# One decoder layer on one core: attention probabilities and the merged sum transposed by VectorE in blocks and through memory

## The chip, the core and the metric

One core of a Trainium2 chip runs the kernel. The metric is the time of one execution on the device in microseconds. The kernel before takes 324.86 us (median of three runs, 324.63 to 325.22).

## The reference

One layer over x (256 tokens, width 1024) with a memory of 256 tokens, all in float32:

```python
h = rms_norm(x, norm_g)
(qa, ka, va, ga, ub, vb, gb, qc, gc, ma, mb, mc) = split_cols(h @ w_in, IN_SPLITS)
out_a = moba_attention(rope(qa), rope(ka), va) * silu(ga)
out_b = gmlp_spatial_gate(ub, vb, ln_g, w_spatial, b_spatial) * silu(gb)
out_c = memory_cross_attention(qc, rms_norm(mem, mem_norm_g), w_mem_kv) * silu(gc)
y = sigmoid(ma) * (out_a @ w_branch_a) + sigmoid(mb) * (out_b @ w_branch_b) + sigmoid(mc) * (out_c @ w_branch_c)
return rms_norm(x + y @ w_out, final_norm_g)
```

Branch a has six heads of 128; with 256 tokens its block-sparse attention is plain causal attention. Branch b normalises vb and mixes it over tokens with a lower triangular matrix for each of six groups in chunks of 128 tokens, and adds a bias. Branch c has four heads that attend to the 256 memory tokens.

## The kernel before

**Chunks.** The weights come as 106 chunks of 128x1024, two to a piece, from three buffers `raw` on SP's DMA queue (`load`, L172). ScalarE makes the high part of a chunk (`hi`, L184) and VectorE the low part (`lo`, L188), three chunks ahead of TensorE, in four buffers of each. TensorE takes three passes (high by high, high by low, low by high) for a chunk. Chunks 0 to 81 are the input projection: `vvb` and `mv` (values), `sig` (the merge gates, four chunks for each 512 columns: sig 1024 and sig 1536 among them), which give token-major sums (L344 to L346), and q, k, gc, ga, ub, qc, mk, gb, which give feature-major ones (L435). Then come 16 chunks of the branch projections and 8 of the output projection.

**PSUM.** Eight banks: four `acc` and four `aux` (`bank`, L149). The sums of a chunk group lie in two acc banks, but those of vvb 1024 and sig 1024 in two aux banks (L366). Scores, transposes, products with V and the spatial mix take one aux bank each.

**Order.** Everything beside the chunks is a unit of the class `Units` (L68): a name, an engine, a duration in us, a function, the units it comes after, a time to wait before its result counts, and a due chunk. `slot` puts a unit into the program ahead of or behind a chunk once the modelled times say that it is ready. So a changed duration or dependency moves the work of all engines.

**Attention.** A head's scores are computed feature-major (`a_scores`, `c_scores`), softmax is done with probabilities `p` (tokens by keys), and the product with V wants them transposed. For heads 0, 1, 4 and 5 of branch a three 128x128 blocks are transposed by TensorE into an aux bank (`a_pT`, L579), for c head 3 four. For heads 2 and 3 of a (`TURN`) and c 0 to 2 VectorE does it in 16 instructions of 32 rows each (`turn_rows`, L571) into `mid`, a buffer in SBUF that the rope uses before. ScalarE then makes `pth` (L662, L771), VectorE `ptl` (L352), and TensorE multiplies (L674). One diagonal block of a needs no low part and is copied to `pt` (L667).

**Around it.** The rope moves q and k by SP's DMAs (L558). The spatial mix of branch b (`mix_unit`, L814) is three units of eight matmuls, each with a bias add on VectorE (`mix_bias`, L822) and then a product on GpSimd. GpSimd also multiplies ub by its gate (L480). The gates of c and a end as `lo` parts of their outputs (L834). The merged sum y, two halves of 512 columns, is transposed by TensorE, 16 blocks (`y_units`, L579), and split. The norm factors of memory go through a diagonal matrix and two matmuls (L288) to a row broadcast on all partitions.

Of the kernel before, what the change touches and what calls it, by code (L numbers as in the profile page):

```python
# [127 lines left out]
def tile_hybrid_layer(ctx: ExitStack, tc: tile.TileContext, xw, memT, mem, x, fin_g, ln_g, w, w_sp, b_sp, rope, out):  # L128
# [439 lines left out]
    def turn_rows(dst, src, a):  # L568

        for b in range(4):  # L570
            nc.vector.transpose(dst(slice(32 * b, 32 * b + 32), slice(32 * a, 32 * a + 32)),  # L571
                                src(slice(32 * a, 32 * a + 32), slice(32 * b, 32 * b + 32)))
# [80 lines left out]
    def a_turn(h, a):
        p = ST["a", h][0][:, 0:384].rearrange("p (m s) -> p m s", m=3)
        ST["ap", h] = V["mid"][:, TURN.index(h), :]
        pt = ST["ap", h][:, 0:384].rearrange("p (m s) -> p m s", m=3)
        turn_rows(lambda r, s: pt[r, :, s], lambda r, s: p[r, :, s], a)

    def a_pT_out(h):
        ps = ST["ap", h]  # L660
        pth = p_tiles("a", h, ps)
        nc.scalar.activation(pth[:, 0:S], ps[:, 0:S], AF.Copy)  # L662
        if h in TURN:
            ST["a1", h] = ps[:, S:S + 128]
            return
        ST["a1", h] = work.tile([128, 128], F32, name="pt1", tag="pt1", bufs=2)
        nc.scalar.activation(ST["a1", h], ps[:, S:S + 128], AF.Copy)  # L667

    def a_pv(h):
# [4 lines left out]
        nc.tensor.matmul(ps[:, 128:256], V["v1"][:, hsl(h)], ST["a1", h], start=False, stop=True)  # L674

    def a_out(h):
        nc.scalar.activation(V["qk"][:, h, 0, :], ST["ao", h][:, 0:S], AF.Copy)
# [21 lines left out]
            (DVE, 0.2, lambda: nc.vector.reciprocal(lrs, lrt)), after=["vvb.1024"])  # L699

    U.add("sqrts", None, 0, lambda: None, after=["lnr", "mrow"])
    U.chain("mrms", *rms_all("m", rstm), after=["mrow"])
    mk0 = chunks.index(("fea", "mk", 0))

    def mem_units():
        U.add("mxa", None, 0, mem_alloc, after=["vvb.1024"])
        for k in range(KD):
# [3 lines left out]
            U.add(f"mxl{k}", DVE, 0.5, lambda k=k, g=g: gain_lo(mem_k(k), g, V["mh"][:, k, :], V["ml"][:, k, :]),  # L711
                  after=[f"mxh{k}"], due=mk0 - 5 + k // 2)

    for h in range(HA):
        if h == 2:
            mem_units()
        if h % 2 == 0:
            r = h // 2
            U.add(f"rin{r}", QUEUE, 1.6, lambda r=r: rope_move(r, False), wait=1.2,
                  after=[f"{n}{i}" for i in (h, h + 1) for n in "qk"] + ["consts"] + ([f"rout{r - 1}"] if r else []))  # L720
            U.add(f"rp{r}", DVE, 1.65, lambda r=r: rope_pair(r), after=[f"rin{r}"])
            U.add(f"rout{r}", QUEUE, 1.6, lambda r=r: rope_move(r, True), after=[f"rp{r}"], wait=1.2)
# [6 lines left out]
        turn = [(DVE, 1.1, lambda h=h, a=a: a_turn(h, a)) for a in range(4)] if h in TURN else \  # L729
            [(PE, 0.33, lambda h=h: a_pT(h))]  # L730
        U.chain(f"ap{h}", *turn, (ACT, 0.42 if h in TURN else 0.72, lambda h=h: a_pT_out(h)),
                after=[f"an{h}"] + back("v", h))
        U.chain(f"av{h}", (DVE, 0.42, lambda h=h: p_lo("a", h, S)), (PE, 0.55, lambda h=h: a_pv(h)),
                (ACT, 0.4, lambda h=h: a_out(h)), after=[f"ap{h}"])
# [26 lines left out]
    def c_turn(h, a):
        if h == 0 and a == 0:
            V["ct"] = V["mid"]
        p = ST["c", h][0].rearrange("p (t m s) -> p m t s", t=2, m=2)
        pt = V["ct"][:, h, :].rearrange("p (m t s) -> p m t s", t=2, m=2)
        turn_rows(lambda r, s: pt[r, :, :, s], lambda r, s: p[r, :, :, s], a)
        ST["cp", h] = V["ct"][:, h, :]
# [348 lines left out]
```

## Time and profile before

| | |
|---|---|
| median of three runs | 324.86 us (324.63 to 325.22) |
| the profiled execution | 325.27 us |
| its span | 323.3 us |
| TensorE busy | 315.8 us, 98% |
| VectorE busy | 246.6 us, 76% |
| ScalarE busy | 202.5 us, 63% |
| GpSimd busy | 40.1 us, 12% |
| DMA | 64.92 MB, 201 GB/s |

All stands for one profiled execution, whose span lies 1.97 us within its time. [...] In a chain of waits each piece is followed back to what released it.

### The profile page before, as it was taken

To read this page: it belongs to the slowest core of one execution; us is meant where nothing else is said; L and a number is where in the kernel's file an instruction comes from. 1 tells how busy PE (TensorE), PEld (TensorE's weight loads), DVE (VectorE), ACT (ScalarE), POOL (GpSimd) and SP (SyncE) were. 2 spreads that over 40 slices of the span, in tenths; PEclk is the share of its full clock that TensorE was granted. 3 is DMA by queue.
4 is the path that set the end of the run, shared out by engine and by line. 5 is a ranking of instruction groups with operands and counts; after the bars stand their busy time and mean duration, and the time that the engine had idled before them with its cause. 6 is when DMAs were issued, how large, how long until landed. Compare 5 with 4: busy or idle time off the path is not lost.

```text
span 323.3 us, 4570 instructions
## 1 busy us (share of the span) xinstructions
PE 315.8 (98%) x1644; PEld 268.9 (83%) x1644; DVE 246.6 (76%) x419; ACT 202.5 (63%) x346; POOL 40.1 (12%) x42
## 2 busy tenths in 40 slices
PE   8999999999999999999999999999999999999992
PEld 3788888888888888898888888888888888888982
DVE  3969956985876999898979639989857659769452
ACT  4879887556865555557677698576746633434433
POOL 1007420000000000030200009200124000000022
PEclk9999999999999999999999999999999999999999
DMA  7999796555327565554544533864640667463003
GB/s 246 419 426 398 258 363 220 216 194 216 136 78 302 172 180 208 164 192 138 185 151 176 195 130 131 312 233 170 208 182 19 244 231 289 150 241 130 0 2 130
DMA packets 13846, 64.92 MB, mean 201 GB/s; under 512 B 1792, under 2 KB 2944, under 8 KB 8576
## 3 DMA queue, kind: packets, MB, share of 16 engines
q1 hardware_dynamic: 13536, 64.31, 55.1%
q10 hardware_dynamic: 288, 0.33, 0.3%
q8 instruction: 13, 0.21, 0.2%
q14 instruction: 9, 0.07, 0.1%
HBM read 62.79 MB, written 1.05 MB: 197 GB/s over the span
## 4 chain that ended last, share of the span: by engine, by line
PE 96%; DMA 2%; ACT 1%; SPq 0%; ACTq 0%; issue 0%; DVE 0%
PE acc L435 36%; PE acc L344 13%; PE acc L345 13%; PE acc L346 13%; PE aux L344 5%; PE aux L345 5%; PE aux L346 5%; PE acc L375 3%; DMA st<-in_xw_dram 2%; PE aux L579 1%; PE aux L814 1%; PE aux L626 0%; PE aux L674 0%; SPq L218 0%; ACT hi L315 0%; PE aux L288 0%
## 5 line engine op out<-in xcount | busy, mean ns | idle before, releaser
L188 DVE TENSOR_TENSOR lo<-raw,hi 128x1024 fp32r<-128x1024 f32 x102 | 130.2, 1280 | 43.0 <-ACT hi L184 42.0
L184 ACT ACTIVATE hi<-raw 128x1024 fp32r<-128x1024 f32 x102 | 107.6, 1056 | 44.3 <-PE acc L346 29.6
L435 PE MATMUL acc<-n,hi 128*128 128x512 f32 x304 | 78.5, 394 | 0.0
L435 PEld LDWEIGHTS acc<-n,hi 128*128 128x128 f32 x304 | 54.8, 189 | 9.5
L435 PEld LDWEIGHTS acc<-n,lo 128*128 128x128 f32 x304 | 41.5, 190 | 3.0
L435 PE MATMUL acc<-n,lo 128*128 128x256 f32 x304 | 42.4, 282 | 0.0
L344 PE MATMUL acc<-hi,n 128*128 128x512 f32 x80 | 31.5, 394 | 0.0
L345 PE MATMUL acc<-lo,n 128*128 128x512 f32 x80 | 31.2, 390 | 0.0
L346 PE MATMUL acc<-hi,n 128*128 128x512 f32 x80 | 31.2, 389 | 0.0
L571 DVE STREAM_TRANSPOSE mid<-p 32x128 f32<-32x128 f32 (+1 forms) x80 | 23.1, 289 | 1.6 <-ACT p L609 0.5
L741 POOL TENSOR_TENSOR vb<-vb,lng 128x768 f32<-128x768 f32 x2 | 4.6, 2276 | 108.4 <-DMA raw<-in_w_dram 94.7
L346 PEld LDWEIGHTS acc<-hi,n 128*128 128x128 f32 x80 | 15.0, 188 | 3.2
L345 PEld LDWEIGHTS acc<-lo,n 128*128 128x128 f32 x80 | 15.0, 188 | 2.9
L344 PEld LDWEIGHTS acc<-hi,n 128*128 128x128 f32 x80 | 15.0, 188 | 2.9
L958 POOL TENSOR_TENSOR xk<-xk,fing 128x512 f32<-128x512 f32 (+1 forms) x4 | 4.0, 1013 | 68.0 <-ACT jk L954 68.0
L516 POOL TENSOR_TENSOR st<-st,bc 128x256 f32<-128x256 f32 x8 | 9.1, 1170 | 24.4 <-ACT bc L293 24.4
L439 ACT ACTIVATE qk<-acc 128x256 f32<-128x256 f32 x12 | 4.6, 380 | 10.7 <-PE acc L435 10.6
L439 ACT ACTIVATE jt<-acc 128x256 f32<-128x256 f32 x14 | 5.3, 377 | 9.0 <-PE acc L435 8.9
L825 POOL TENSOR_TENSOR qk<-qk,ga 128x512 f32<-128x512 f32 x3 | 5.8, 1966 | 33.8 <-ACT ga L801 33.8
L375 PE MATMUL acc<-hi,h 128*128 128x512 f32 (+1 forms) x34 | 8.9, 386 | 0.9 <-ACT hi L315 0.9
L344 PE MATMUL acc<-hi,a 128*128 128x512 f32 x24 | 9.4, 393 | 0.0
L346 PE MATMUL acc<-hi,a 128*128 128x512 f32 x24 | 9.3, 389 | 0.0
(233 smaller groups left out, 601.2 us busy)
## 6 DMA issues: line engine op xcount, KB each, us to landing
raw<-in_w_dram SPq DMA_DIRECT2D x39, 1024.0 KB, 4.9
raw<-in_w_dram SPq DMA_DIRECT2D x24, 512.0 KB, 4.6
st<-in_xw_dram SPq DMA_DIRECT2D x6, 384.0 KB, 7.2
xk<-in_x_dram SPq DMA_DIRECT2D x2, 1024.0 KB, 9.1
mt<-in_memT_dram SPq DMA_DIRECT2D x2, 512.0 KB, 7.8
mm<-in_mem_dram SPq DMA_DIRECT2D x2, 512.0 KB, 9.8
out_dram<-xk SPq DMA_DIRECT2D x4, 256.0 KB, 2.7
fing<-in_fin_g_dram SPq DMA_DIRECT2D x1, 512.0 KB, 6.9
```

The lines of the kernel that those rows point to most:

```text
L184: nc.scalar.activation(hi[c][:, a:b], raw[c // 2][:, o + a:o + b], AF.Copy)
L188: nc.vector.tensor_tensor(lo[c][:, a:b], raw[c // 2][:, o + a:o + b], hi[c][:, a:b].bitcast(F32), OP.subtract)
L344: nc.tensor.matmul(p, s_hi, m_hi, start=first, stop=False)
L345: nc.tensor.matmul(p, s_hi, m_lo, start=False, stop=False)
L346: nc.tensor.matmul(p, s_lo, m_hi, start=False, stop=last)
L375: nc.tensor.matmul(acc[name, o][t][:, a:b], src[:, k, tsl(t)], wt[c][:, i * 512 + a:i * 512 + b], start=k + n == 0, stop=k == KD - 1 and n ...
L435: nc.tensor.matmul(o, wt, m, start=i == 0, stop=i == len(passes) - 1)
L439: nc.scalar.activation(dst, pa, AF.Copy)
L516: U.add(f"nm{k}", POOL, 1.05, lambda k=k: nc.gpsimd.tensor_tensor(x_k(k), x_k(k), bc["x"], OP.mult), after=["xrms"], due=7)
L571: nc.vector.transpose(dst(slice(32 * b, 32 * b + 32), slice(32 * a, 32 * a + 32)), src(slice(32 * a, 32 * a + 32), slice(32 * b, 32 * b + ...
L741: nc.gpsimd.tensor_tensor(V["vb"][:, t, :], V["vb"][:, t, :], V["lng"], OP.mult)
L825: nc.gpsimd.tensor_tensor(src, src, g, OP.mult)
```

## The change

All ten heads, memory's norm factors and three quarters of y are transposed without TensorE. `turn_blocks` is one VectorE instruction that transposes every 32x32 block in place of its row of blocks; `turn_write` writes the result in four DMAs from SP to a scratch tensor in memory, in runs of 32n floats, in the order that completes the transpose; `turn_read` reads it back by one DMA that ScalarE issues. The result has its columns in another order, which `turn_view` undoes when `pth` and `ptl` are made. The third block of an a head is read straight from there, without a copy. All heads share one buffer for the write, `mid[:, 0]`, one after another (`moved`), and two for the read. The first half of y and one of two token tiles of the second go the same way; the other tile takes four TensorE transposes. The norm factors are written as a row and read back as a broadcast. Pieces 31 and 32 come in halves too, the rope's modelled waits go from 1.2 to 2.4 and 1.6, and the due time of the c scores is gone.

```diff
-        parts = 2 if 20 <= j < 31 else 1
+        parts = 2 if 20 <= j < 33 else 1
...
+    def rms_write(name, r):
+        bc["r" + name] = row = dram.tile([S], F32, name="row" + name)
+        nc.sync.dma_start(bass.AP(tensor=row.tensor, offset=row.offset, ap=[[1, 128], [128, 2]]), r)
+
+    def rms_read(name):
+        bc[name] = work.tile([128, S], F32, name="bc", tag="ssq", bufs=2)
+        nc.sync.dma_start(bc[name], rows(bc["r" + name], S))
...
+    def turn_blocks(dst, src):
+        nc.vector.transpose(dst, src.rearrange("p (u b j) -> p b u j", b=4, j=32))
+
+    def turn_write(name, src, n):
+        ST["d" + name] = d = dram.tile([128, 128 * n], F32, name="turn" + name)
+        w = 32 * n
+        for a in range(4):
+            nc.sync.dma_start(bass.AP(tensor=d.tensor, offset=d.offset + a * w, ap=[[4 * w, 32], [128 * w, 4], [1, w]]),
+                              src[32 * a:32 * a + 32].rearrange("p (b w) -> p b w", b=4))
+
+    def turn_read(name, dst):
+        nc.scalar.dma_start(dst, ST["d" + name])
+
+    def turn_view(t, a, b):
+        return t.rearrange("p (a u i) -> p u a i", a=4, i=32)[:, a:b]
...
-    TURN = (2, 3)
+    TURN_A, TURN_C = (0, 1, 2, 3, 4, 5), (0, 1, 2, 3)
...
-    U.chain("mrms", *rms_all("m", rstm), after=["mrow"])
+    U.add("mrmw", QUEUE, 0.4, lambda: rms_write("m", rstm), after=["mrow"], wait=9.0)
+    U.add("mrms", QUEUE, 0.4, lambda: rms_read("m"), after=["mrmw"], wait=4.0)
...
+    def turn_units(kind, h, n, i):
+        name = f"{kind}{h}"
+        before = [f"{kind}n{h}"] + moved[0]
+        U.add(f"tt{name}", DVE, 0.2 + 0.13 * n, lambda: p_turn(kind, h, n), after=before)
+        U.add(f"tw{name}", QUEUE, 1.6, lambda: turn_write(name, V["mid"][:, 0, 0:128 * n], n), after=[f"tt{name}"], wait=3.6)
+        U.add(f"{kind}pt{h}", ACT, 0.45, lambda: p_back(kind, h, n), after=[f"tw{name}"] + back("v", i), wait=3.2)
+        moved[0] = [f"tw{name}"]
...
-                after=[f"qcl{h | 1}", f"mkl{h | 1}", "sqrts"] + back("p", HA + h), due=n_in - 26 + h)
+                after=[f"qcl{h | 1}", f"mkl{h | 1}", "sqrts"] + back("p", HA + h))
...
-                for i in range(2):
-                    y_units(half, i, [f"y{c}"])
+                if half == 0:
+                    part = y_turn(0, [0, 1], [f"y{c}"], ("yw0", "ub"), ("yr0", "gc"), 4.0)
+
+                    U.add("yp0", ACT, 1.3, part, after=["yr0"], due=n_br - 2)
+                else:
+                    y_turn_pe([f"y{c}"])
+                    V["ylast"] = y_turn(1, [1], [f"y{c}"], ("yw1", "ub"), ("yr1", "gc"), 2.0)
```

Over the whole program TensorE has 1600 matmuls in place of 1630 (four transposes in place of 32, two in place of four for norm factors), VectorE 351 instructions in place of 418, and SP 164 in place of 112.

**TensorE around the spatial mix.** Before, the last matmuls of a chunk of sig 1536, the mix, and the next chunk (`aux_2485`, `aux_2490`, `aux_2495` are the three groups' banks, `wsp` the spatial weights):

```order
L344 MATMUL acc_2472<-hi_2386,n_168 128x512
L345 MATMUL acc_2472<-lo_2387,n_168 128x512
L346 MATMUL acc_2472<-hi_2386,n_168 128x512
L814 MATMUL aux_2485<-wsp_161,vb_284 128x128 [waits Pool_49] x2
L814 MATMUL aux_2485<-wsp_161,vb_284 128x128 x2
L814 MATMUL aux_2490<-wsp_161,vb_284 128x128 x4
L814 MATMUL aux_2495<-wsp_161,vb_284 128x128 [waits Activation_49]
L814 MATMUL aux_2495<-wsp_161,vb_284 128x128 x3
L344 MATMUL acc_2471<-hi_2410,n_168 128x512
```

Now, the mix behind the third chunk of sig 1024 (`aux_2192` and `aux_2193` hold its sums; `aux_2253`, `aux_2258` and `aux_2263` are the mix's):

```order
L353 MATMUL aux_2193<-hi_2159,n_170 128x512
L354 MATMUL aux_2193<-lo_2160,n_170 128x512
L355 MATMUL aux_2193<-hi_2159,n_170 128x512
L877 MATMUL aux_2253<-wsp_163,vb_286 128x128 [waits Pool_49] x2
L877 MATMUL aux_2253<-wsp_163,vb_286 128x128 x2
L877 MATMUL aux_2258<-wsp_163,vb_286 128x128 x4
L877 MATMUL aux_2263<-wsp_163,vb_286 128x128 [waits DVE_49,PE_49]
L877 MATMUL aux_2263<-wsp_163,vb_286 128x128 x3
L353 MATMUL aux_2192<-hi_2186,n_170 128x512 [waits Activation_49]
```

The mix moved from the sums of sig 1536, in acc banks, into those of sig 1024, in aux banks, and the third group's first matmul waits for VectorE in place of ScalarE.

**VectorE around the bias adds of the mix.** Before (`lo` are low parts of weight chunks, `ptl` those of probabilities, `mt` the bias adds):

```order
L188 TENSOR_TENSOR lo<-raw,hi 128x1024
L834 TENSOR_TENSOR ocl<-oc,och 128x512
L188 TENSOR_TENSOR lo<-raw,hi 128x1024 x2
L352 TENSOR_TENSOR ptl<-aux,pth 128x512
L822 TENSOR_TENSOR mt_2501<-aux,bsb 128x256 x2
L822 TENSOR_TENSOR mt_2504<-aux,bsb 128x256 x2
L822 TENSOR_TENSOR mt_2507<-aux,bsb 128x256 x2
L188 TENSOR_TENSOR lo<-raw,hi 128x1024
```

Now (`a` are the low parts of branch a's gated outputs):

```order
L189 TENSOR_TENSOR lo<-raw,hi 128x1024
L897 TENSOR_TENSOR a<-qk,a 128x2x256 x3
L189 TENSOR_TENSOR lo<-raw,hi 128x1024 x2
L361 TENSOR_TENSOR ptl<-mid,pth 128x256 x4
L885 TENSOR_TENSOR mt_2272<-aux,bsb 128x256 x2
L885 TENSOR_TENSOR mt_2275<-aux,bsb 128x256 x2
L189 TENSOR_TENSOR lo<-raw,hi 128x1024
L885 TENSOR_TENSOR mt_2315<-aux,bsb 128x256 x2
```

The first two groups' bias adds now stand behind three chunks' low parts, those of branch a's outputs and the four of c heads 2 and 3; before, they stood behind one c head's low part.

**ScalarE around heads 0 and 1 of branch a.** Before (`gc` are copies out of the gc chunks, `pth` the high parts of probabilities, `qk` the outputs of heads):

```order
L184 ACTIVATE hi<-raw 128x1024
L439 ACTIVATE gc<-acc 128x256
L662 ACTIVATE pth<-aux 128x256
L667 ACTIVATE pt_898<-aux 128x128
L184 ACTIVATE hi<-raw 128x1024
L439 ACTIVATE gc<-acc 128x256
L662 ACTIVATE pth<-aux 128x256
L667 ACTIVATE pt_931<-aux 128x128
L184 ACTIVATE hi<-raw 128x1024
L439 ACTIVATE gc<-acc 128x256
L677 ACTIVATE qk<-aux 128x256 x2
```

Now, three gc chunks further on:

```order
L185 ACTIVATE hi<-raw 128x1024
L448 ACTIVATE gc<-acc 128x256
L594 DMA mid<-turna_946 128x384
L185 ACTIVATE hi<-raw 128x1024
L448 ACTIVATE ub<-acc 128x256
L641 ACTIVATE qh<-qk 128x384 x2
L698 ACTIVATE pth<-mid 128x256
L185 ACTIVATE hi<-raw 128x1024
L448 ACTIVATE ub<-acc 128x256
```

The high part of head 0 stood right behind the first gc copy; now the first of the reads (`mid<-turna`) stands behind the fourth, and the high part of head 0 after one more chunk, with high parts of weight chunks in front and behind.

## Rows read from the trace of the kernel before

**Rows 1.** Table by stretch: us, PE, PEld, DVE, ACT, POOL busy, clock, DMA share, GB/s.

```profile
17.00:312.00 295.00, 295.00 (x1551) 253.70 (x1550) 231.06 (x388) 186.99 (x314) 36.32 (x31) 1.00 0.55 197
```

**Rows 2.** Chain of waits: start us, us, engine, tile, line, count.

```profile
63.66 0.24 PE aux L288 x2
63.91 8.38 PE acc L435 x48
81.82 0.33 PE aux L579 x3
163.04 0.65 PE aux L579 x6
235.09 0.44 PE aux L579 x4
277.11 0.87 PE aux L579 x8
```

**Rows 3.** Timeline, TensorE, 200 to 202 us: start us, us, then the group.

```profile
200.81 0.40 PE L344 MATMUL aux<-hi,n 128*128 128x512 f32 x1
201.96 0.39 PE L346 MATMUL aux<-hi,n 128*128 128x512 f32 x1
```

**Rows 4.** Timeline, TensorE, 237 to 242 us.

```profile
238.14 2.84 PE L814 MATMUL aux<-wsp,vb 128*128 128x128 f32 x24
240.74 0.48 PE L344 MATMUL acc<-hi,n 128*128 128x512 f32 x1
```

**Rows 5.** Timeline, VectorE, 191 to 211 us; in brackets idle before and releaser.

```profile
194.28 1.50 DVE L188 TENSOR_TENSOR lo<-raw,hi 128x1024 fp32r<-128x1024 f32 x1 [1.03 <-ACT hi L184]
196.03 2.00 DVE L188 TENSOR_TENSOR lo<-raw,hi 128x1024 fp32r<-128x1024 f32 x1
204.03 1.22 DVE L188 TENSOR_TENSOR lo<-raw,hi 128x1024 fp32r<-128x1024 f32 x1
205.17 2.98 DVE L834 TENSOR_TENSOR a<-qk,a 128x512 fp32r<-128x512 f32 x3
208.07 3.49 DVE L188 TENSOR_TENSOR lo<-raw,hi 128x1024 fp32r<-128x1024 f32 x3
```

**Rows 6.** Timeline, VectorE, about 165 and 239 us.

```profile
165.13 0.75 DVE L352 TENSOR_TENSOR ptl<-aux,pth 128x256 fp32r<-128x256 f32 x2
239.23 2.54 DVE L822 TENSOR_TENSOR mt<-aux,bsb 128x256 f32<-128x256 f32 x6 [0.27 <-PE aux L814]
```

**Rows 7.** Timeline, GpSimd, 185 to 210 us.

```profile
193.38 5.81 POOL L825 TENSOR_TENSOR qk<-qk,ga 128x512 f32<-128x512 f32 x3 [33.78 <-ACT ga L801]
199.17 3.53 POOL L480 TENSOR_TENSOR ub<-ub,jt 128x512 f32<-128x512 f32 x2
205.46 1.53 POOL L480 TENSOR_TENSOR ub<-ub,jt 128x512 f32<-128x512 f32 x1 [2.76 <-ACT jt L479]
```

**Rows 8.** Groups by line and shape, VectorE, line 571: total us, mean ns, idle before.

```profile
L571 DVE STREAM_TRANSPOSE mid<-p 32x128 f32<-32x128 f32 x48 | 14.5, 302 | 0.7
L571 DVE STREAM_TRANSPOSE mid<-p 32x96 f32<-32x96 f32 x32 | 8.6, 270 | 0.9 <-ACT p L609 0.5
```

**Rows 9.** DMA issues (ns min/median/max) and landings (us), lines 558 and 218; a DMA row.

```profile
L558 SPq DMA_DIRECT2D mid<-qk x12: 507/555/1064, 48.4 to 112.2; - x12
DMA to landing us min/median/max: 1.7/3.3/6.0
L218 ACTq DMA_DIRECT2D st<-in_xw_dram x2: 414/432/451, 0.8 to 1.2; - x2
st<-in_xw_dram ACTq DMA_DIRECT2D x1, 192.0 KB, 3.6
```

**Rows 10.** Waits of SP's queue: total us, times, longest us.

```profile
SPq L170 <- DVE lo L188: 156.4, 33, 9.8
```

**Rows 11.** Timeline, TensorE, 97 to 99 us, two groups of scores.

```profile
97.49 0.38 PE L626 MATMUL aux<-qk 128*128 128x128 f32 x2
98.64 1.54 PE L435 MATMUL acc<-n,hi 128*128 128x512 f32 x6
```

More of the change, by code (lines that the diff above doesn't have):

```diff
@@ L134, in tile_hybrid_layer @@
     work = ctx.enter_context(tc.tile_pool(name="work", bufs=2))
+    dram = ctx.enter_context(tc.tile_pool(name="dram", bufs=1, space=bass.MemoryType.DRAM))
     psum = ctx.enter_context(tc.tile_pool(name="psum", bufs=1, space=PSUM))
@@ L566, in rope_pair @@
         nc.vector.tensor_tensor(x, x, sh, OP.add)
[L568 to L572, printed above, removed]
-    TURN = (2, 3)
+    def turn_blocks(dst, src):
[11 more added lines that the diff above has]
+    TURN_A, TURN_C = (0, 1, 2, 3, 4, 5), (0, 1, 2, 3)
     def transpose4(p, blocks):
@@ L651, in a_pT, with p_turn, p_back, p_lo_turned @@
         transpose4(ST["ap", h], [p[:, hsl(j)] for j in range(3)])
[L653 to L657, printed above, removed]
+    def p_turn(kind, h, n):
+        turn_blocks(V["mid"][:, 0, 0:128 * n].rearrange("p (b u j) -> p b u j", b=4, j=32),
+                    ST[kind, h][0][:, 0:128 * n])
+    def p_back(kind, h, n):
+        t = V["mid"][:, 1 + h % 2, 0:128 * n]
+        turn_read(f"{kind}{h}", t)
+        ST[kind + "p", h] = t
+    def p_lo_turned(kind, h, n):
+        ps, pth, ptl = ST[kind + "T", h]
+        sub_lo(ptl[:, 0:128 * n].rearrange("p (u a i) -> p u a i", a=4, i=32), turn_view(ps, 0, n),
+               pth[:, 0:128 * n].rearrange("p (u a i) -> p u a i", a=4, i=32))
     def a_pT_out(h):
@@ L661, in a_pT_out @@
         pth = p_tiles("a", h, ps)
+        if h in TURN_A:
+            nc.scalar.activation(pth[:, 0:S].rearrange("p (u a i) -> p u a i", a=4, i=32), turn_view(ps, 0, 2),
+                                 AF.Copy)
+            ST["a1", h] = turn_view(ps, 2, 3)[:, 0]
+            return
         nc.scalar.activation(pth[:, 0:S], ps[:, 0:S], AF.Copy)
-        if h in TURN:
-            ST["a1", h] = ps[:, S:S + 128]
-            return
         ST["a1", h] = work.tile([128, 128], F32, name="pt1", tag="pt1", bufs=2)
@@ L673, in a_pv @@
         mm3(ps[:, 0:S], v0[:, 0, hsl(h)], v0[:, 1, hsl(h)], pth[:, 0:S], ptl[:, 0:S], True, False)
-        nc.tensor.matmul(ps[:, 128:256], V["v1"][:, hsl(h)], ST["a1", h], start=False, stop=True)
+        p1, o1 = ST["a1", h], ps[:, 128:256]
+        if h in TURN_A:
+            o1 = o1.rearrange("p (a i) -> p a i", a=4)
+        nc.tensor.matmul(o1, V["v1"][:, hsl(h)], p1, start=False, stop=True)
     def a_out(h):
@@ L712, in mem_units @@
                   after=[f"mxh{k}"], due=mk0 - 5 + k // 2)
+    moved = [[]]
+    def turn_units(kind, h, n, i):
[5 more added lines that the diff above has]
+        moved[0] = [f"tw{name}"]
     for h in range(HA):
@@ L718, in tile_hybrid_layer @@
             r = h // 2
-            U.add(f"rin{r}", QUEUE, 1.6, lambda r=r: rope_move(r, False), wait=1.2,
+            U.add(f"rin{r}", QUEUE, 1.6, lambda r=r: rope_move(r, False), wait=2.4,
                   after=[f"{n}{i}" for i in (h, h + 1) for n in "qk"] + ["consts"] + ([f"rout{r - 1}"] if r else []))
             U.add(f"rp{r}", DVE, 1.65, lambda r=r: rope_pair(r), after=[f"rin{r}"])
-            U.add(f"rout{r}", QUEUE, 1.6, lambda r=r: rope_move(r, True), after=[f"rp{r}"], wait=1.2)
+            U.add(f"rout{r}", QUEUE, 1.6, lambda r=r: rope_move(r, True), after=[f"rp{r}"], wait=1.6)
         U.chain(f"qsl{h}", (ACT, 0.5, lambda h=h: a_split_hi(h)), (DVE, 0.55, lambda h=h: a_split_lo(h)),
@@ L728, in tile_hybrid_layer @@
                 after=[f"as{h}"])
[L729 to L733, printed above, removed]
+        if h in TURN_A:
+            turn_units("a", h, 3, h)
+        else:
+            U.add(f"apt{h}", PE, 0.33, lambda h=h: a_pT(h), after=[f"an{h}"])
+        U.add(f"ap{h}", ACT, 0.42 if h in TURN_A else 0.72, lambda h=h: a_pT_out(h), after=[f"apt{h}"] + back("v", h))
+        low = (lambda h=h: p_lo_turned("a", h, 2)) if h in TURN_A else (lambda h=h: p_lo("a", h, S))
+        U.chain(f"av{h}", (DVE, 0.42, low), (PE, 0.55, lambda h=h: a_pv(h)),
                 (ACT, 0.4, lambda h=h: a_out(h)), after=[f"ap{h}"])
@@ L759, in c_pT, with c_lo @@
         transpose4(ST["cp", h], [p[:, hsl(j)] for j in (0, 2, 1, 3)])
[L761 to L767, printed above, removed]
     def c_pT_out(h):
         ps = ST["cp", h]
-        nc.scalar.activation(p_tiles("c", h, ps), ps, AF.Copy)
+        pth = p_tiles("c", h, ps)
+        if h in TURN_C:
+            for m in range(2):
+                nc.scalar.activation(pth[:, m * S:m * S + S].rearrange("p (u a i) -> p u a i", a=4, i=32),
+                                     turn_view(ps, 0, 4)[:, m::2], AF.Copy)
+            return
+        nc.scalar.activation(pth, ps, AF.Copy)
+    def c_lo(h):
+        if h not in TURN_C:
+            return p_lo("c", h, 512)
+        ps, pth, ptl = ST["cT", h]
+        for m in range(2):
+            o, i = (x[:, m * S:m * S + S].rearrange("p (u a i) -> p u a i", a=4, i=32) for x in (ptl, pth))
+            sub_lo(o, turn_view(ps, 0, 4)[:, m::2], i)
     def c_pv(h):
@@ L788, in tile_hybrid_layer @@
                 (ACT, 1.15, lambda h=h: softmax_exp("c", h)),
-                after=[f"qcl{h | 1}", f"mkl{h | 1}", "sqrts"] + back("p", HA + h), due=n_in - 26 + h)
+                after=[f"qcl{h | 1}", f"mkl{h | 1}", "sqrts"] + back("p", HA + h))
         U.chain(f"cn{h}", (DVE, 0.2, lambda h=h: softmax_sum("c", h)), (ACT, 0.85, lambda h=h: softmax_norm("c", h)),
                 after=[f"cs{h}"])
-        turn = [(DVE, 1.25, lambda h=h, a=a: c_turn(h, a)) for a in range(4)] if h < 3 else             [(PE, 0.44, lambda h=h: c_pT(h))]
-        U.chain(f"cp{h}", *turn, (ACT, 0.62, lambda h=h: c_pT_out(h)), after=[f"cn{h}"] + back("v", HA + h))
-        U.chain(f"cv{h}", (DVE, 0.68, lambda h=h: p_lo("c", h, 512)), (PE, 0.72, lambda h=h: c_pv(h)),
+        if h in TURN_C:
+            turn_units("c", h, 4, HA + h)
+        else:
+            U.add(f"cpt{h}", PE, 0.44, lambda h=h: c_pT(h), after=[f"cn{h}"])
+        U.add(f"cp{h}", ACT, 0.75, lambda h=h: c_pT_out(h), after=[f"cpt{h}"] + back("v", HA + h))
+        U.chain(f"cv{h}", (DVE, 0.84, lambda h=h: c_lo(h)), (PE, 0.72, lambda h=h: c_pv(h)),
                 (ACT, 0.4, lambda h=h: c_out(h)), after=[f"cp{h}", "mvl0", "mvl1"])
@@ L879, in tile_hybrid_layer, with y_parts, y_turn, blocks @@
     BR = [("a", k) for k in range(HA)] + [("b", k) for k in range(GB)] + [("c", k) for k in range(HC)]
-    def y_units(half, i, after):
-        k = slice(4 * half + 2 * i, 4 * half + 2 * i + 2)
+    def y_parts(half, ts, src):
+        k, s = slice(4 * half, 4 * half + 4), slice(128 * ts[0], 128 * ts[-1] + 128)
+        h, l = (V[n][:, k, s].rearrange("p k (t a i) -> p k t a i", t=len(ts), a=4) for n in ("yh", "yl"))
+        for t in range(len(ts)):
+            nc.scalar.activation(h[:, :, t], src[:, :, t], AF.Copy)
+            nc.vector.tensor_tensor(l[:, :, t], src[:, :, t], h[:, :, t].bitcast(F32), OP.subtract)
+    def y_turn(half, ts, after, to, back, us):
+        n = 4 * len(ts)
+        shape = [128, 4, len(ts), 128]
+        def blocks():
+            slot_tile(to[0], shape, to[1])
+            for i, t in enumerate(ts):
+                turn_blocks(V[to[0]][:, :, i, :].rearrange("p b (u j) -> p b u j", j=32), sig[half][:, t, :])
+        def write():
+            turn_write(f"y{half}", V[to[0]].rearrange("p b t x -> p (b t x)"), n)
+        def read():
+            slot_tile(back[0], shape, back[1])
+            turn_read(f"y{half}", V[back[0]].rearrange("p a t x -> p (a t x)"))
+        U.add(f"yw{half}", DVE, 0.75 * len(ts), blocks, after=after)
+        U.add(f"yx{half}", QUEUE, 1.6, write, after=[f"yw{half}"], wait=us)
+        U.add(f"yr{half}", ACT, 0.45, read, after=[f"yx{half}"], wait=3.2)
+        return lambda: y_parts(half, ts, V[back[0]].rearrange("p a t (k i) -> p k t a i", i=32))
+    def y_turn_pe(after):
         def turn():
-            ST["y", half, i] = bank()
-            transpose4(ST["y", half, i], [sig[half][:, t, hsl(2 * i + a)] for a in range(2) for t in range(2)])
-            split2(ST["y", half, i].rearrange("p (k s) -> p k s", k=2), V["yh"][:, k, :], V["yl"][:, k, :])
+            ST["y"] = bank()
+            transpose4(ST["y"], [sig[1][:, 0, hsl(k)] for k in range(4)])
+            y_parts(1, [0], ST["y"].rearrange("p (k t a i) -> p k t a i", k=4, t=1, a=4))
             U.run(DVE, 0.7, U.run(ACT, 0.62, U.t[PE]))
-        U.add(f"yt{half}{i}", PE, 0.44, turn, after=after)
+        U.add("yt", PE, 0.44, turn, after=after)
     def mm_br(c):
@@ L1013, in tile_hybrid_layer @@
         split(c0 + LEAD)
+    V["ylast"]()
     for col in range(2):
```

1 line of the change is left out of this document (added).

## Prediction

> **What bounds the kernel now.** I read the table by stretch first, then the chain of waits, then the timelines of single engines. [...] The sum is made against the profiled execution, 325.27 us; its distance to the median of 324.86 (0.41 us) is carried over unchanged.
>
> **What leaves TensorE.** Each piece is a row of the chain [rows 2]: norm factors of memory 0.24; heads a 0 and 1, three transposes each, 0.33 twice (81.82 and a like row at 84.97); heads a 4 and 5 together 0.65; c head 3, four, 0.44; merged sum y, 16, 0.87 twice (277.11 and a like row at 299.76). That is 3.73 us. Four of the 16 for y remain (half of a 0.87 piece, 0.44). Removed: **3.29 us**. Alone it would give 324.86 - 3.29 = 321.57 us.
>
> [...]
>
> **A wait that the change adds.** The order of the work moves too, and this is the term that I chose with most care. The spatial mix (three groups of eight matmuls, one auxiliary PSUM bank each) stood before inside the sums of sig 1536, which are in acc banks. Now it stands after the third of the four chunks of sig 1024, whose two sums hold two of the four auxiliary banks. Two are left for three groups, so the third group takes the bank of the first and must wait until VectorE has added the bias to it; the order shows that wait on VectorE, where before it was one on ScalarE whose work was long done. Behind the waiting matmul stand the last chunk of sig 1024 and all that follows on TensorE.
>
> When does each side arrive? On the time axis of before: chunk 66, the first of sig 1024, starts at 200.81 [rows 3]; it is 12 matmuls, which start 0.23 us apart (six starts from 200.81 to 201.96), so 2.76 us, and three end at 209.1. Two of the three groups of the mix take two thirds of the 2.60 us from 238.14 to 240.74 [rows 4], so TensorE stands at the bank at 210.8. VectorE has, ahead of that bias add, the low parts of chunks 69 to 71, the three low parts of branch a's outputs, four low parts for c heads 2 and 3, and the four adds of the first two groups, of which the first two must end. Before, the low parts ran 204.03, 205.17 to 208.07, and 208.07 on at 1.16 us each [rows 5], so that of chunk 71 ends at about 210.40. Then four low parts of 128x256 at 0.75 us for two [rows 6], 1.50, and two adds at 2.54/6 [rows 6], 0.85: VectorE is done at 212.75. The wait is **about 2.0 us** by these rows alone.
>
> Two things lengthen it. The gate products of ub on GpSimd stood two at 199.17 to 202.70 and one at 205.46 [rows 7]; now all three fall into the stretch before the bias add. Beside a product of GpSimd (193.38 to 199.19, [rows 7]) low parts took 1.50 and 2.00 us, against 1.22 without one [rows 5]: 1.06 more in 3.50 us, 0.3 us for each us. The two products that come to lie here are 3.53 us, so about +1.0. And ScalarE must first make the four high parts for heads 2 and 3 in the same stretch, with up to 1 us more. I take **3.0 us**, between 2.0 and 4.0: VectorE's contention is on rows of the same two operations, ScalarE's share only argued.
>
> **Sum.** -3.29 + 3.0 = -0.29: 324.98 for the profiled execution, **324.6 us** for the median. With both ends, 323.6 to 325.6.
>
> **What I cost at nothing, and its cover.** VectorE loses 80 block transposes, 14.5 + 8.6 = 23.1 us [rows 8]. It gains 13 whole ones: six of 384 columns, four and three of 512. A 32x128 one takes 0.302, a 32x96 one 0.270 [rows 8], 0.032 for each 32 columns; carried on in that line 384 columns take 0.56 and 512 take 0.69, by the whole duration for each 128 columns 0.91 and 1.21. So 8 to 14 us come back, and I take 8, since the two rows show that columns are the smaller part of a duration. Nothing waits for that. ScalarE issues 12 reads at about 0.43 [rows 9] = 5.2 us and loses four copies; it is idle for 108 us of the stretch [rows 1]. SP issues 48 writes at 0.56 [rows 9] = 27 us, plus two for the norm row, and loses its freedom to issue a weight load at once; but it waits 156.4 us for the weight buffers to come free [rows 10], and a write that stands ahead of a load delays it by 0.6 to 2.3 us (one or four issues). If a write waits long for its transpose, a load behind it waits too; that cover ends only where TensorE has used up the chunks loaded ahead, and the price is then the delay itself. The bytes, 2.9 MB out and as much back (six heads of 192 KB, four of 256, 512 and 256 for y), add 10% to the 58 MB of the stretch (197 GB/s), whose DMA share is 0.55 [rows 1]. The norm factors go out and back while four chunks run, over 10 us against two landings of at most 6.0 [rows 9]. The loads of pieces 31 and 32 in halves, the longer plan times of the rope and the due time of the c scores that goes move only work that is covered.
>
> **The round trips** (transpose, write, read, high part, low part, then the product with V) must land in time. The tightest is head 0: its read is issued about 0.8 us after the chunk whose gc copy stands ahead of it, and the product stands two chunks and two score groups later. Two chunks are two thirds of 8.38 [rows 2], 5.6; two score groups are 98.64 - 97.49 = 1.15 [rows 11]; together 6.7 us, less 0.8 for the start and 1.0 for the high and low part and their handoffs, leaves 4.9. The nearest reads: 192 KB on ScalarE's queue 3.6; the rope's moves 1.7 / 3.3 / 6.0 [rows 9]. So 3.6 fits, 6.0 misses by 1.1. I take 3.6, the nearest in size and queue, though a 1 MB weight load runs beside it.
>
> **Rivals.**
> 1. *VectorE arrives in time*, or nearly: the wait is at most 2 us, and 321.6 to 323.6 comes out. For it: 15 us of work leave VectorE, which had 64 us idle in the stretch [rows 1]. Against it: a low part can't run ahead of its high part, and that waits for a buffer that TensorE frees, so VectorE is tied to TensorE's place and the idle time is not there to be saved up. Chance 0.21.
> 2. *The reads land late* (slower). ScalarE waits in its own order for the data of head 0 before the high part, and the high parts of weight chunks stand behind it, so TensorE loses first its product and then its next chunk. It decides once a read takes more than 4.9 us from issue. Price: 1.1 at 6.0 for the product, up to as much again on the weight chunk behind it, and 1.0 if the head with the next smallest room, 4, misses as well: 324.6 + 1.1 to 3.2 = 325.7 to 327.8. For it: the spread to 6.0 with far fewer bytes, and a concurrent weight load. Against it: 3.6 at this very size. Chance 0.20.
> 3. *Small pieces make every trip slow.* A write moves runs of 32n floats, 384 to 1024 bytes. At 6.0 us for each of twelve reads, 12 x 1.1 = 13 us: about 338. Against it, the rope's moves are in small pieces too and their median is 3.3 [rows 9]. Chance 0.04. [...]
>
> **How the numbers follow.** A measurement of this kernel tells no less than about 0.2%, 0.65 us: "same" is 324.21 to 325.51. The forecast (wait of 2 to 4, trips fit) has 0.55: 0.18 of it faster, 0.34 same, 0.03 slower, since most of 323.6 to 325.6 lies inside the bound. With rival 1 faster, rivals 2 and 3 slower: faster 0.39, same 0.34, slower 0.27. The range 322.4 to 327.0 leaves out the lower two fifths of rival 1 (0.08), the upper two fifths of rival 2 (0.08) and rival 3 (0.04); the likeliest case's own range is 323.6 to 325.6.
>
> **What would show it.** TensorE's matmul count is down by 30 and its rows hold four transposes in place of 32; one idle piece of 2 to 4 us before the third mix group, released by VectorE's bias add, and no other above 0.5; reads landing in 3 to 4.5 us; VectorE's transposes at 0.4 to 1.2 each. The prediction is wrong if that piece is under 1 us, if TensorE waits ahead of products with V or of weight chunks, or if TensorE's time shrinks by other than 3.3.

## The result and the profile after

The changed kernel takes 327.39 us (median of 12 runs, 325.75 to 329.84), the kernel before 324.83 beside it: a ratio of 1.009 (of the means), with an interval of 1.0078 to 1.0102. One of the twelve runs of the kernel before took 821.46 us and is left out of the ratio. By the medians the changed kernel is **slower by 2.56 us**, where 324.6 and a range of 322.4 to 327.0 stood in the prediction. The profiled execution took 327.19 us, 1.92 more than before, and has a span of 325.5 us, 2.2 more than before.

The page of the changed kernel, then its table by stretch (columns as in [rows 1]):

```profile
PE 315.0 (97%) x1614; PEld 267.9 (82%) x1614; DVE 229.6 (71%) x352; ACT 202.3 (62%) x345; POOL 41.9 (13%) x42
...
PEclk9999999999999999999999999979999999999998
```

```profile
17.00:312.00 295.00, 291.54 (x1512) 250.29 (x1511) 213.70 (x320) 186.06 (x311) 36.86 (x30) 0.99 0.66 218
```

TensorE was busy for 295.00 of 295.00 us [rows 1]; now 3.46 us are missing, and a slice of the granted clock (the row PEclk, in tenths of full speed) reads 7, where the page of before has 9 in all forty. Fewer matmuls, and yet TensorE's busy time fell by only 0.8 us over the span: some of them ran slower. The waits of TensorE, in total us, times and longest, the longest one of before first, then those of the changed kernel:

```profile
PE acc L375 <- ACT hi L315: 0.9, 1, 0.9
```

```profile
PE aux L877 <- DVE mt L885: 3.5, 1, 3.5
PE aux L251 <- PEq L1202: 0.8, 1, 0.8
PE acc L384 <- ACT hi L324: 0.3, 1, 0.3
```

There is one new wait in the program, the forecast one, before the third group of the spatial mix. The chain of waits leaves TensorE just there (start us, us, what):

```profile
204.20 0.88 DVE a L897
...
205.91 3.47 DVE a L897 x2
209.38 2.27 DVE lo L189 x2
211.65 1.34 DVE ptl L361 x4
212.99 0.68 DVE mt L885 x2
...
213.81 1.94 PE aux L877 x8
215.74 0.43 PE aux L353
216.17 0.43 PE aux L354
216.59 0.43 PE aux L355
217.02 0.43 PE aux L353
217.45 0.25 PE aux L354
217.69 0.23 PE aux L355
...
302.35 0.44 PE aux L605 x4
```

On VectorE the instructions come in the order that the prediction read: low parts of branch a's outputs, two low parts of chunks, four of c heads, the adds. What the prediction doesn't have is the part behind 213.81. Eight matmuls of the mix take 1.94 us, where a third of the group of before [rows 4] was 0.87; four matmuls of 512 columns take 0.43 each, where they took 0.23 [rows 3]. The table by stretch says why; its last three columns are the granted clock, the DMA share and GB/s:

```profile
212.00:213.00 1.00, 0.00 (x0) 0.00 (x0) 1.00 (x4) 0.00 (x0) 0.00 (x0) 1.00 0.40 49
213.00:214.00 1.00, 0.20 (x1) 0.23 (x2) 1.00 (x4) 0.00 (x0) 0.20 (x1) 0.97 0.64 262
214.00:215.00 1.00, 1.00 (x6) 1.00 (x6) 1.00 (x2) 0.00 (x0) 1.00 (x1) 0.50 0.93 393
...
216.00:217.00 1.00, 1.00 (x4) 0.81 (x3) 0.81 (x3) 0.00 (x0) 1.00 (x1) 0.50 0.00 0
217.00:218.00 1.00, 1.00 (x6) 0.77 (x4) 0.00 (x0) 0.00 (x0) 1.00 (x2) 0.83 0.00 0
218.00:219.00 1.00, 1.00 (x6) 0.84 (x5) 0.00 (x0) 0.31 (x1) 0.54 (x1) 1.00 0.00 0
```

TensorE had stood from 210.35 to 213.81. About 0.1 us after its restart (the 0.97 of that slice) the granted clock fell to 0.50, and it came back to 1.00 at about 217.3 (the 0.83 of that slice), after TensorE had worked for 3.5 us. In that piece the work took 1.94 - 0.87 = 1.07, four times 0.43 - 0.23 = 0.80, and 0.02 more than at a clock of 1.00, 1.9 us in all. Not all of this is the clock: in two kernels below the same eight matmuls take 1.13 at a clock of 1.00, behind a wait of 1.09 us and right behind other matmuls alike. So 0.26 is not the clock (the 1.13 runs to the end of the last matmul, the 0.87 to the next start), and 1.6 is. The ledger of the profiled execution is then -3.29 + 3.46 + 1.9 = +2.07, and 325.27 + 2.07 = 327.3 us, where 327.19 was measured.

The lines that the prediction's other steps rest on: transposes on VectorE (total us, mean ns of one), DMA rows (KB each, median us to landing), the landings of the reads (line 594), and the waits of SP's queue:

```profile
L582 DVE STREAM_TRANSPOSE mid<-p 128x384 f32<-128x384 f32 x6 | 3.4, 572 | 0.0
L582 DVE STREAM_TRANSPOSE mid<-p 128x512 f32<-128x512 f32 x4 | 2.8, 710 | 0.1
```

```profile
mid<-turna ACTq DMA_DIRECT2D x6, 192.0 KB, 4.1
...
mid<-turnc ACTq DMA_DIRECT2D x4, 256.0 KB, 3.4
...
bc<-rowm SPq DMA_DIRECT2D x1, 128.0 KB, 8.9
rowm<-rstm SPq DMA_DIRECT2D x1, 1.0 KB, 8.8
```

```profile
DMA to landing us min/median/max: 2.3/3.9/7.3
```

```profile
SPq L171 <- DVE lo L189: 109.2, 24, 12.0
```

A whole transpose takes 0.57 or 0.71 us (0.56 and 0.69 were forecast), the heads' reads land in 3.4 to 4.1 in the median, the slowest in 7.3, and TensorE waits for none of them. One row is out of line: the norm factors' 1 KB, written as 256 pieces of four bytes, takes 8.8 us to land.

### The profile page after: what moved, and what is told of

The parts are those of the page before. It is cut to its first block, busy times and chain, and to the rows that moved or that the text cites. A ratio compares the mean times of both kernels' runs of the same rounds, so it can differ in the third digit from the quotient of the medians.

```text
span 325.5 us, 4554 instructions
## 1 busy us (share of the span) xinstructions
PE 315.0 (97%) x1614; PEld 267.9 (82%) x1614; DVE 229.6 (71%) x352; ACT 202.3 (62%) x345; POOL 41.9 (13%) x42
## 4 chain that ended last, share of the span: by engine, by line
PE 92%; DVE 3%; DMA 2%; ACT 1%; issue 1%; SPq 0%; ACTq 0%
PE acc L444 36%; PE acc L353 13%; PE acc L355 13%; PE acc L354 13%; PE aux L353 4%; PE aux L354 4%; PE aux L355 4%; PE acc L384 3%; DMA st<-in_xw_dram 2%; DVE a L897 1%; DVE lo L189 1%; PE aux L877 1%; DVE ptl L361 0%; PE aux L652 0%; PE aux L714 0%
## 5 line engine op out<-in xcount | busy, mean ns | idle before, releaser
L189 DVE TENSOR_TENSOR lo<-raw,hi 128x1024 fp32r<-128x1024 f32 x102 | 128.0, 1258 | 67.4 <-ACT hi L185 64.2
L355 PE MATMUL acc<-hi,n 128*128 128x512 f32 x80 | 31.1, 389 | 0.0
L796 POOL TENSOR_TENSOR vb<-vb,lng 128x768 f32<-128x768 f32 x2 | 5.4, 2714 | 109.0 <-DVE vb L793 86.3
L355 PEld LDWEIGHTS acc<-hi,n 128*128 128x128 f32 x80 | 15.0, 188 | 3.2
L361 DVE TENSOR_TENSOR ptl<-mid,pth 128x256 fp32r<-128x256 f32 x14 | 7.1, 535 | 3.4 <-ACT pth L698 2.9
L354 PE MATMUL acc<-lo,a 128*128 128x512 f32 x24 | 9.3, 389 | 0.0
L355 PE MATMUL acc<-hi,a 128*128 128x512 f32 x24 | 9.3, 389 | 0.0
L353 PE MATMUL acc<-hi,obh 128*128 128x512 f32 x24 | 9.3, 389 | 0.0
```

The costliest lines, as they stand in the source:

```text
L189: nc.vector.tensor_tensor(lo[c][:, a:b], raw[c // 2][:, o + a:o + b], hi[c][:, a:b].bitcast(F32), OP.subtract)
L353: nc.tensor.matmul(p, s_hi, m_hi, start=first, stop=False)
L354: nc.tensor.matmul(p, s_hi, m_lo, start=False, stop=False)
L355: nc.tensor.matmul(p, s_lo, m_hi, start=False, stop=last)
L361: nc.vector.tensor_tensor(dl, p, dh.bitcast(F32), OP.subtract)
L796: nc.gpsimd.tensor_tensor(V["vb"][:, t, :], V["vb"][:, t, :], V["lng"], OP.mult)
```

## The experiments

Theory: the wait at the mix's third group, and the fall of the clock that TensorE's standing there brings, ate what the removed matmuls gave. Rivals: the ways through memory (the write to the scratch tensor and the read back) cost time somewhere else; the clock falls for another reason than the wait. The first four kernels ran beside a kernel before at 324.69 us, the other four beside one at 325.00.

**Sums of sig 1024 in acc banks** (same order of instructions):

```diff
-            acc[name, o] = [bank(), bank()] if o == 1024 else [acc_bank(), acc_bank()]
+            acc[name, o] = [bank(), bank()] if o == 1024 and name == "vvb" else [acc_bank(), acc_bank()]
```

> The changed kernel with the sums of sig 1024 in two acc banks, so that all three groups of the spatial mix find a free aux bank; the order of the instructions is the same on every engine. Theory (the one new wait of 3.46 us before the third mix group and the granted clock of 0.50 in the 3.4 us behind it, some 1.9 us, have eaten the 3.29 us): no wait, clock 1.00 from 17 to 312 us, 327.4 - 3.5 - 1.9 = 322.0 us, 321.6 to 322.6. Rival 1 (the ways through memory and their traffic cost time elsewhere, the wait only takes up slack): 324.5 or more, with TensorE idle or slower in other places. Rival 2 (the clock falls because of the mix's small matmuls or of the load on the chip there, not because of the wait): clock 0.50 behind the mix still, 323.9.

Measured: 323.03 us, ratio 0.9945 (0.9931 to 0.9959). No wait at the mix, its 24 matmuls in one run, the clock at 1.00 through the stretch (columns as above):

```profile
210.00:214.00 4.00, 4.00 (x30) 3.71 (x29) 4.00 (x7) 0.85 (x1) 0.00 (x0) 1.00 0.22 66
```

Two banks make 4.4 us between the two kernels' medians, and the order is the same. But 323.03 is above the expected 321.6 to 322.6: TensorE has a new wait, for the rope, and 0.2 more behind it:

```profile
PE aux L652 <- DMA qk<-mid: 0.7, 1, 0.7
```

Behind the rope the theory can be read by itself: from the first L355 matmul in the rope's first scores to the first product with V behind the mix are 146.5 us in the changed kernel (72.59 to 219.13) and 141.2 here (73.72 to 214.95). That is 5.3 us, against the 5.4 of the theory.

**The mix behind sig 1024**, banks as they were:

```diff
-                after=["lna0", "lna1", f"cp{HC - 1}"])
+                after=["lna0", "lna1", f"cp{HC - 1}", f"c{sig2 + 1}"])
```

> The changed kernel with the mix moved behind the chunk after sig 1024 (one more name in its list of what it comes after), banks as they were. Theory: as with the acc banks, no wait above 0.5 us, clock 1.00, 322.0 us, 321.6 to 322.8. Rival 1 (cost elsewhere): 324.5 or more. Rival 2 (clock falls by the mix itself): 323.9.

Measured: 322.52 us, ratio 0.9932 (0.992 to 0.9945), as the theory has it; no wait at the mix, clock 1.00. Both ways of taking the wait away bring the clock back with it, in one of them (the acc banks) with the mix at its place: its 24 small matmuls ran at a clock of 1.00 there, so they are not what lowers it. The rope's landing is late here too; the list of waits shows 0.2 us for it on TensorE, and 0.2 behind.

**Without GpSimd's gate products.** This leaves out the multiplication of ub by its gate.

```diff
-                        (POOL, 1.6, lambda: nc.gpsimd.tensor_tensor(u, u, g, OP.mult)),
+                        (POOL, 1.6, lambda: None),
```

> The changed kernel without GpSimd's three products of ub with its gate (left out, the planner's times unchanged): VectorE's three low parts of branch a's outputs then have no GpSimd beside them, 5.18 -> about 3.0 us, and the wait before the third mix group shrinks from 3.46 to 1.0 to 1.5 us. If the clock's fall hangs on how long TensorE stood: clock stays 1.00 and 327.4 - 2.3 - 1.9 = 323.2. If any wait there brings it: 325.1, clock 0.50 for some us. Rival (the wait is set by ScalarE or by a read, not by VectorE under GpSimd): the wait stays above 3 and so does the time, 327.4.

Measured: 324.02 us, ratio 0.9976 (0.9966 to 0.9985). The timelines of VectorE and TensorE (start us, us; in brackets idle before), and a line of the table by stretch:

```profile
205.01 1.89 DVE L897 TENSOR_TENSOR a<-qk,a 128x512 fp32r<-128x512 f32 x3
```

```profile
212.24 1.13 PE L877 MATMUL aux<-wsp,vb 128*128 128x128 f32 x8 [1.09 <-DVE mt L885]
```

```profile
212.00:214.00 2.00, 1.76 (x12) 1.66 (x13) 2.00 (x4) 0.00 (x0) 1.83 (x2) 1.00 1.00 418
```

Three low parts take 1.89 us with nothing on GpSimd, 2.98 with one product beside them [rows 5], 5.18 (204.20 to 209.38) with three products of 5.21 us in all. The wait shrinks to 1.09, and the eight matmuls behind it take 1.13 in place of 1.94: after this shorter wait the clock stayed at 1.00. The time is 0.8 above the expected 323.2, which had not counted the rope's wait (0.7 + 0.2 in this profile's list as well).

**A longer wait.** The first add of the first mix group is done nine times:

```diff
-            nc.vector.tensor_tensor(tmp[:, a], pv[:, a], b, OP.add)
+            for _ in range(9 if i == 0 and a == 0 else 1):
+                nc.vector.tensor_tensor(tmp[:, a], pv[:, a], b, OP.add)
```

> The changed kernel with the first bias add of the first mix group done nine times (eight more of about 0.34 us): the wait grows from 3.46 to about 6.2 us. If the clock's cost is a fixed 1.9: 330.1. If it grows with the wait: 331 to 332. If the fall has nothing to do with the wait: the time grows by the 2.7 alone and the clock's piece lies where it lay in program order, 330.1 too, but then the kernels without a wait show it as well.

Measured: 332.11 us, ratio 1.0234 (1.021 to 1.0257); the wait is 7.14 us, from 210.0 to 217.15, where 6.2 was expected. The clock by stretch:

```profile
210.00:212.00 2.00, 0.01 (x1) 0.00 (x0) 2.00 (x5) 0.00 (x0) 0.00 (x0) 1.00 0.02 8
212.00:214.00 2.00, 0.00 (x0) 0.00 (x0) 1.90 (x7) 0.00 (x0) 0.00 (x0) 0.72 0.88 217
...
216.00:218.00 2.00, 0.85 (x4) 0.88 (x5) 1.97 (x6) 0.00 (x0) 0.85 (x1) 0.50 0.00 0
218.00:220.00 2.00, 2.00 (x9) 1.81 (x9) 2.00 (x3) 0.00 (x0) 2.00 (x2) 0.50 0.00 0
220.00:222.00 2.00, 2.00 (x7) 1.52 (x6) 0.16 (x1) 0.00 (x0) 1.88 (x2) 0.50 0.00 0
222.00:224.00 2.00, 2.00 (x9) 1.69 (x8) 0.00 (x0) 0.89 (x1) 0.00 (x0) 0.72 0.00 0
```

The clock falls inside the idle piece, with no matmul running (0.72 from 212 to 214, then 0.50), and stays down until TensorE has worked for some 6 us (217.15 to about 223.1, by the last 0.72). 7.42 us over the kernel before, less 7.14 - 3.29 = 3.85, leaves 3.6. By the rows the clock's share of this is 3.0: the 6 us of work from 217.15 to about 223.1 at half speed. The rope takes 0.7 more than in the changed kernel (see below). So the price grew with the wait, as the second of the expected outcomes had it (332.11 lies just past its 331 to 332); a fixed 1.9 would have given 324.69 + 3.85 + 1.9 = 330.4.

**TensorE kept busy in the wait.** The changed kernel, wait and all, with 15 matmuls that nobody reads in front of the third group:

```diff
+        if i == 2:
+            d, c = acc_bank(), max(hi) - LEAD
+            for n in range(15):
+                nc.tensor.matmul(d, V["nh"][:, n % KD, tsl(0)], hi[c][:, 0:512], start=n == 0, stop=n == 14)
```

> The changed kernel as it is, with 15 matmuls of 512 columns (3.4 us) on TensorE between the second and the third group of the mix, into an acc bank that nobody reads: TensorE works while it would wait. Theory (the clock fell because TensorE stood idle): the wait is under 0.8 us, the granted clock stays 1.00 and 327.4 - 1.9 = 325.5 to 326.2 us. Rival (the clock falls by the load or by the mix's small matmuls): clock 0.50 as before, 327.4 or more.

Measured: 325.48 us, ratio 1.0017 (1.0008 to 1.0026): 1.9 us faster than the changed kernel with 15 matmuls more, at the lower edge of the expected 325.5 to 326.2. The timeline of TensorE and the table by stretch:

```profile
210.58 3.66 PE L875 MATMUL acc<-hi,n 128*128 128x512 f32 x15
214.29 1.13 PE L881 MATMUL aux<-wsp,vb 128*128 128x128 f32 x8
```

```profile
214.00:216.00 2.00, 1.95 (x14) 1.60 (x13) 1.39 (x4) 1.06 (x1) 1.71 (x2) 1.00 0.93 389
```

The third group starts at the same place in the program and a little later in time than in the changed kernel (214.29 against 213.81), and then runs at 1.00. This is the cleanest of the tests: VectorE's work, GpSimd's work, the DMAs and the place are as they were, only the standing still is gone. Over the kernel before it is 0.48 us slower, the change 2.56: by these medians **what the standing adds to its own length is about 2.1 us**, near the 1.9 of the rows, of which 1.6 is the clock; the wait's own length and the removed matmuls about cancel.

**Memory's norm factors on TensorE again**, with the mix behind sig 1024:

```diff
-    U.add("mrmw", QUEUE, 0.4, lambda: rms_write("m", rstm), after=["mrow"], wait=9.0)
-    U.add("mrms", QUEUE, 0.4, lambda: rms_read("m"), after=["mrmw"], wait=4.0)
+    U.chain("mrms", *rms_all("m", rstm), after=["mrow"])
```

> The changed kernel with the mix behind sig 1024 and memory's norm factors on TensorE again as before (0.24 us of matmuls back); the mix then stands in the sums of sig 1536, as before. Theory: in the kernels without the mix's wait the norm row's write (256 pieces of 4 bytes, 9 to 10 us to land, the DMA at 20 to 84 GB/s meanwhile) makes the rope's first DMAs land late, and TensorE's first scores wait 0.2 to 0.9 us for them. Here the rope lands in at most 6 us, no such wait, and 322.5 + 0.24 - 0.5 = 322.2 us (321.8 to 322.6), closer together than the 322.0 to 323.0 of the kernel with the row. Rival (the rope is late because of other traffic): its wait stays, 322.8.

Measured: 321.75 us, ratio 0.9902 (0.9888 to 0.9915), 321.62 to 321.92, so closer together and a little better than expected. The rope's landings, line 567, in this kernel:

```profile
DMA to landing us min/median/max: 1.7/4.0/5.4
```

In the kernel with the row and the mix moved they go up to 11.7. The DMA at the same place, 60 to 64 us, first in that kernel, then here:

```profile
60.00:64.00 4.00, 4.00 (x23) 3.44 (x22) 2.75 (x4) 2.36 (x4) 0.00 (x0) 1.00 0.76 27
```

```profile
60.00:64.00 4.00, 4.00 (x24) 3.49 (x23) 3.43 (x8) 2.69 (x6) 0.00 (x0) 1.00 0.60 243
```

A busier DMA that moves a ninth of the bytes: 1 KB in 256 pieces holds up what runs beside it. What it costs TensorE is more than the list of waits says, since a matmul of 512 columns is listed at 0.39 us where the next starts 0.23 us behind it, and an idle piece shorter than that overlap doesn't show. In the kernel with the row and the mix moved, the chain of waits and the starts of TensorE's matmuls around the rope's first scores are:

```profile
60.34 11.39 DMA qk<-mid
```

```profile
71.22 0.39 PE L444 MATMUL acc<-n,hi 128*128 128x512 f32 x1
71.86 0.46 PE L652 MATMUL aux<-qk 128*128 128x128 f32 x2 [0.24 <-DMA qk<-mid]
...
73.20 0.28 PE L355 MATMUL aux<-qh,ql 128*128 128x256 f32 x1
```

From the last matmul of the chunk to the last of these rows are 1.98 us (71.22 to 73.20). The kernel before takes 0.69 for the same, this kernel 0.70, the changed one 0.91, those with the wait filled or made longer 1.50 and 1.58, and those with acc banks or without gate products 2.45 and 2.46.

**The norm row written from ScalarE's queue**, with the mix behind sig 1024:

```diff
-        nc.sync.dma_start(bass.AP(tensor=row.tensor, offset=row.offset, ap=[[1, 128], [128, 2]]), r)
+        nc.scalar.dma_start(bass.AP(tensor=row.tensor, offset=row.offset, ap=[[1, 128], [128, 2]]), r)
...
-    U.add("mrmw", QUEUE, 0.4, lambda: rms_write("m", rstm), after=["mrow"], wait=9.0)
+    U.add("mrmw", ACT, 0.4, lambda: rms_write("m", rstm), after=["mrow"], wait=9.0)
```

> The changed kernel with the mix behind sig 1024 and the norm row's write issued by ScalarE on its queue in place of SP's. If the row holds up what stands behind it on the same queue: the rope's DMAs and the weight loads on SP's queue land as in the kernel before (at most 6 us), and 322.0. If the 4-byte pieces occupy the DMA engines themselves: the rope's landing still reaches 10 us and more, the stretch stays under 100 GB/s, and 322.5 as with SP.

Measured: **321.36 us**, ratio 0.989 (0.9876 to 0.9903), the fastest of all kernels here. Neither expected picture holds whole: the row takes 10.3 us on this queue too, the rope's landings still reach 9.5, and 60 to 64 us still move 31 GB/s:

```profile
60.00:64.00 4.00, 4.00 (x23) 3.48 (x22) 2.76 (x3) 2.55 (x5) 0.00 (x0) 1.00 0.56 31
```

But the slow stretch begins four us later (234 GB/s from 56 to 60, where SP's row left 35 in the changed kernel), and TensorE doesn't wait for the rope (0.70 for the scores as read above). Over the kernel with the row on SP's queue (322.52) this is 1.2 us by the medians, and the rope's scores account for 1.98 - 0.70 = 1.3. So what runs on the other queue is held up too (the rope's 9.5 us, the 31 GB/s); by what it is held up no run shows.

**The ten heads alone**, mix behind sig 1024, y and the norm factors by TensorE: the functions of y and the line of the norm factors are those of before.

> The ten heads alone through memory, mix behind sig 1024; y and the norm factors by TensorE as before. Theory: 1.74 us leave TensorE, no wait, clock 1.00: 324.7 - 1.74 = 323.0 (322.7 to 323.4), and 1.30 over the kernel with y through memory as well. Rival 1 (y through memory gives less than its 1.30 because the ends of y arrive later): the difference to that kernel is under 0.7. Rival 2 (heads cost something by reads that land late): over 323.8.

Measured: 323.23 us, ratio 0.9948 (0.9936 to 0.9961): 1.77 us gained where 1.74 of matmuls left. Against the kernel with y through memory as well (321.75) y gives 1.48, for 1.30 of matmuls. So the ways through memory deliver what they take off TensorE.

## Why the prediction was wrong

**What leaves TensorE: right.** 3.29 us was the sum, taken off the time one for one because TensorE had no idle time in the stretch [rows 1]; the four transposes that stay take the forecast 0.44; without the wait and with the row out of SP's way the kernel is 3.64 faster, with 0.24 of it left on TensorE 3.25, and the heads alone give 1.77 for 1.74.

**A wait that the change adds: right in place, cause and nearly in size.** It was put at 210.8 to 213.75, and it lies at 210.35 to 213.81: 3.46 us for 3.0. The extra is TensorE being there 0.45 earlier. VectorE was done when forecast, but by two errors that cancel, which is luck: "about +1.0" for two more products of GpSimd was too little, since the low parts of branch a's outputs alone took 5.18 in place of 2.98, and VectorE began them 1.0 earlier (204.20 for 205.17). ScalarE's share, argued at up to 1, shows no wait.

**The step that failed is the price of that wait**, "-3.29 + 3.0 = -0.29". It counted the wait by its length and let TensorE go on behind it at the clock of before. No row of the kernel before shows TensorE standing for more than 0.9 us, and the granted clock of 1.00 [rows 1] was read as a constant. In its place: 3.46 us of standing and 1.9 us more for the work behind it, 1.6 of them by the clock of 0.50 (about 2.1 by the kernel that fills the wait). With these 1.9 the same sum gives 324.6 + 1.9 = 326.5, with the measured wait 327.0; the rest to the median of 327.39 lies inside the spread of the runs.

The spread of the changed kernel's runs, 4.1 us against 0.8 before, fits a price of this kind: from the shortest to the longest the mean granted clock goes from 0.996 to 0.988, 0.008 of 325 us, 2.6 of the 4.1. The runs of the kernel before have 0.994 to 0.999 (those beside the experiments), so in the shortest run, at 0.996, the clock may hardly have fallen in the wait; no profile of that run shows it. What sets the rest was not tried.

**What was costed at nothing.** VectorE's, ScalarE's and SP's work was covered as argued: TensorE waits for none of it in the changed kernel except at the mix. The norm row was wrong: "two landings of at most 6.0" were 8.8 and 8.9, taken from the rope's moves, whose pieces are larger than four bytes. TensorE waited for neither of its two landings, but the rope behind it came late. By the starts of the matmuls that cost TensorE 0.2 us in the changed kernel, and 0.8 to 1.8 in the other kernels with the row on SP's queue.

**Rivals.** VectorE did not arrive in time. No read landed too late for TensorE: head 0's was issued at 91.36 and its high part started at 94.17, without a wait. The slowest read, the fourth of branch a's six, took 7.3 us, outside the 3 to 4.5 that the prediction named; ScalarE waited 3.2 us in all for reads of branch a, and TensorE not at all. Small pieces made no trip of the heads slow (writes 4.5 and 2.2 us in the median, reads 4.1 and 3.4); the one slow transfer in small pieces was the norm row, 8.8 us.

## What to carry to other kernels

A wait on the engine that bounds the kernel can cost more than its length: here the clock fell to 0.50 at waits of 3.46 and 7.14 us, and the work behind them ran at that for 3.4 and some 6 us. Price that too, or fill the wait. When work is moved by a planner that doesn't know buffers, look for the groups that no longer find a free one: here three groups met two banks, and one more name in a list of dependencies turned +2.56 us into -2.2. A transfer of few bytes can take long: here 1 KB in four-byte pieces took 8.8 us in the changed kernel.

## What was not expected of the hardware

The granted clock fell to 0.50 with a standing of 3.46 us, and not with one of 1.09 us; 15 useless matmuls in the place of the standing made the kernel 1.9 us faster (327.39 to 325.48). A write of 1 KB as 256 pieces took 8.7 to 10.3 us to land on either queue, and left 18 to 84 GB/s to all the DMA for about 10 us on SP's and 31 GB/s for 4 us on ScalarE's. Three subtractions on VectorE took 1.89, 2.98 and 5.18 us with none, one and three products of GpSimd beside them.
